# In-projection of a hybrid decoder layer: the low part of a weight tile from a DMA that adds the tile to its negated high part

## The chip, the cores and the metric

The kernel runs on one core of one Trainium2 chip. The metric is device time in microseconds (us) of one execution; less is better. TensorE (PE) does the matrix products, VectorE (DVE), ScalarE (ACT) and GpSimd (POOL) the elementwise work, and DMAs are issued by SyncE (SP) and POOL and carried by 16 DMA engines.

## The reference

One inference step of one decoder layer on 512 prompt tokens and 8 x 4 sample tokens, 544 columns in all, in float32:

```
h    = rms_norm(x, norm_mix_w)
proj = h @ w_in                      # 2048 x (7 * 1024 + 16): B_a | C_a | h_a | q | k | v | z | a | b
y_a  = rms_norm(B_a * dwconv3(C_a * h_a))                    # 8 groups of 128 channels
q, k, v = silu(dwconv4(q | k | v)), q and k L2-normalised
o    = gated_delta_rule(q, k, v, g(a), beta(b), state)       # 8 heads, chunkwise, exact
x    = x + concat(y_a, rms_norm(o) * silu(z)) @ w_out
x    = x + square(relu(rms_norm(x) @ w_up)) @ w_down         # 2048 x 8192 x 2048
y    = rms_norm(x, final_norm_w)
```

The outputs are y and the new convolution and delta states.

## The kernel before, in words

Activations lie transposed, features over 128 partitions and the 544 token columns in two halves of 272. A float32 product is made from numbers that PE takes in one pass: each operand is split into a high part, rounded to the type `fp32r`, and a low part, the rest. A product is then three: high x high, high x low, low x high (`product`).

The in-projection makes 56 slabs of 128 output features. The first three (`N_START`) are made from `w_first` while the input is still coming in. The other 53 are made one after the other, each from two weight tiles of 128 x 1024 (`w_in`, 106 tiles; the loop over `srcs`, with the tile's slab `s` and half `hf`). A tile holds 8 blocks of 128 x 128, and a block is used in 6 matmuls (3 products, 2 column halves), so a tile is 48 matmuls: for each block the two of `x_hi,w_hi`, the two of `x_lo,w_hi`, the two of `x_hi,w_lo`.

`ahead` calls `weight` two tiles ahead of the one that PE uses. `weight` loads a tile into `w_raw` (two buffers) from SP's queue, rounds it on ACT into `w_hi` (three buffers), and DVE subtracts, `w_lo = w_raw - w_hi` (three buffers).

A finished slab goes to a job: `scale_out` reads the sums on DVE, then there is a convolution (`conv`, DVE), an activation (`silu`, ACT), small copies of state on POOL (`qkv_slab`, `c_slab`, `h_slab`, `b_slab`), or a gate (`z_slab`). The 56 slabs come in four groups of 14, two heads with their q, k, v, two convolution groups, and two gates. Beside the slabs of one group runs the delta rule of the group whose q, k, v are done (`delta`, `delta_sample`, `decays`, `scalars`); these are generators, and `run_side` lets each put a few small matmuls between the slabs' own, after every second block. At a group's end `delta` normalises its output (`nk`: a logarithm and an exponential on ACT, a product on DVE, then the product with the gate on POOL, into `tmp`, and a DMA to `cat`).

Tile's scheduler orders each engine's instructions by priority and by when they could start; within `urgent()` the priority is higher, and all of `weight` stands in it. PE's order is nearly that of the program. An engine works in order: where one instruction waits, those behind it wait too. That is also true of POOL's DMA issues.

The rest of the program, the out-projection and the MLP, comes behind the in-projection (from about 830 us) and has its own weights.

Of the kernel before, what the change touches and what calls it, by code (L numbers as in the profile page):

```python
# [9 lines left out]
F32 = mybir.dt.float32  # L10
# [3 lines left out]
AF = mybir.ActivationFunctionType  # L14
ALU = mybir.AluOpType
MUL, ADD, SUB, MIN, MAX = ALU.mult, ALU.add, ALU.subtract, ALU.min, ALU.max
# [31 lines left out]
def ahead(items, load, depth=2):  # L48

    items, queue = list(items), []  # L50
    for i, it in enumerate(items):
        while len(queue) < min(depth + 1, len(items) - i):
            queue.append(load(items[i + len(queue)]))
        yield it, queue.pop(0)
# [3 lines left out]
def trunk(ctx, tc, a):  # L58
    nc = tc.nc
    V, S, G = nc.vector, nc.scalar, nc.gpsimd  # L60
# [34 lines left out]
    def tile_in(p, name, shape, dt=F32, tag=None, bufs=None):  # L95
        return p.tile(shape, dt, tag=tag or name, name=name, bufs=bufs)
# [17 lines left out]
    def urgent():  # L114
        return tc.high_priority(offset=WPRIO)
# [12 lines left out]
    def ps_big():  # L128
        t = tile_in(big, "ps_big", [P, 2, 512], tag="big")
        return [t[:, h, :HT] for h in range(2)], t[:, :, :HT]  # L130
# [1 line left out]
    def ps_small(n=512):  # L132
        return tile_in(small, "ps_sm", [P, 512], tag="sm")[:, :n]

    def weight(src, n, between=None):

        with urgent():
            raw = tile_in(rawp, "w_raw", [P, 1024])
            hi = tile_in(whip, "w_hi", [P, 1024], F32R)
            lo = tile_in(wlop, "w_lo", [P, 1024], F32R)  # L140
            for c in [slice(0, n)] if between is None else [slice(0, n // 2), slice(n // 2, n)]:
                nc.sync.dma_start(raw[:, c], src[:, c])
                S.activation(hi[:, c], raw[:, c], AF.Copy)  # L143
                if between and not c.start:
                    between()
                V.tensor_tensor(lo[:, c], raw[:, c], hi[:, c].bitcast(F32), SUB)  # L146
        return hi, lo

    def split(src, col):
# [14 lines left out]
    def product(ps, w, c, x, start, stop, halves=(0, 1)):  # L164

        (whi, wlo), (xhi, xlo) = w, x
        for i, (wp, xp) in enumerate(((whi, xhi), (whi, xlo), (wlo, xhi))):
            for h in halves:
                x = xp[h] if isinstance(xp, tuple) else xp[:, h, :]
                PE.matmul(ps[h], wp[:, c : c + P], x, start=start and i == 0, stop=stop and i == 2)  # L170
# [32 lines left out]
    with ExitStack() as mix:  # L203
# [33 lines left out]
        for kp in range(KT // 2):  # L237
# [24 lines left out]
            if kp == KT // 2 - 1:  # L262
                square_of(0)
                square_of(1)
            w = weight(a["w_first"][kp], 2 * N_START * P, None if kp else first)
            if kp == 0:
                with urgent():
# [578 lines left out]
        def run_side(drain=False):  # L846
            for item in list(side):
                if item[0] > 0 and not drain:
                    item[0] -= 1
                    continue  # L850
                while True:
                    try:
                        PE.step = True
                        item[0] = next(item[1]) - 1
                    except StopIteration:
                        side.remove(item)
                        break
                    if not drain:
                        break
            PE.step = False  # L860
# [31 lines left out]
            next(jobs)(first_ps[i])  # L892
        side.append([0, scalars()])
        srcs = [(s, hf) for s in range(56 - N_START) for hf in range(2)]
        for (s, hf), w in ahead(srcs, lambda it: weight(a["w_in"][2 * it[0] + it[1]], 1024)):
            if hf == 0:
                job = next(jobs)
                ps = ps_big()
            for k in range(8):
                kk = 8 * hf + k  # L900
                product(ps[0], w, k * P, h_x[kk], kk == 0, kk == KT - 1)
                if k % 2:
                    run_side()
            if hf == 1:
                job(ps)
# [19 lines left out]
        def add(out, ps):  # L925
            with urgent():
                V.tensor_tensor(out, out, ps, ADD)  # L927

        firsts = ahead([(o, q) for o in range(KT) for q in range(2)],
                       lambda it: weight(a["w_o1"][2 * it[0] + it[1]], N1 // 2 * P))  # L930

        def first_part(last, between):
# [36 lines left out]
    def t_tile(name, tag, dt=F32):  # L969
        return tile_in(tt, name, [P, 4, HT], dt, tag=tag, bufs=2 if tag == "u" else 1)  # L970

    def c_tile(p, name):
        return tile_in(p, name, [P, 2, HT], F32R, tag="hl" if p is hlp else "c")
# [57 lines left out]
    for (m, q), w in ahead(steps, step_weight):  # L1031
# [34 lines left out]
        if m in KEPT:  # L1066
            hi = t_tile("u_hi", "hi", F32R)
# [198 lines left out]
    while any(s < len(KS) for s in at):  # L1266
        for m in range(8):
            n = min(SPAN, len(KS) - at[m])
# [22 lines left out]
    for v, (m, k0, n) in enumerate(visits):  # L1291
        c = slice(KS[k0] * P, (KS[k0] + n) * P)
# [12 lines left out]
    for m in STORED:  # L1305
# [3 lines left out]
        for i in range(2):  # L1309
            hi, lo = c_tile(hlp, "ul"), c_tile(hlp, "ul")  # L1310
# [186 lines left out]
```

## Time and profile before

| | |
|---|---|
| time, median of 3 runs (lowest to highest) | 2399.78 us (2398.15 to 2400.69) |
| time of the profiled execution | 2399.76 us |
| its span, first to last instruction | 2398.0 us |
| busy, share of the span | PE 99%, DVE 75%, ACT 44%, POOL 19% |
| granted TensorE clock | 0.998 |
| in-projection tiles, first and last load | 27.4 and 758.8 us |

A profile page gives each engine's busy time, the chain of work that ended last, groups of instructions by line, and the DMA queues. Queries of the trace narrow these to a window of time. In a row such as `w_lo<-w_raw,w_hi` the output stands left of the arrow and the inputs right of it, by the program's names; L146 is line 146 of the kernel. "Idle before" is time in which the engine had nothing to do, and the name behind it what ended it.

### The profile page before, as it was taken

The page shows a single profiled execution, that of the slowest core. Times are in us where ns is not written, and L with a number is a line of the kernel's source. Part 1 is how long each engine was busy: PE and PEld are TensorE (multiplying, and loading weights), DVE is VectorE, ACT ScalarE, POOL GpSimd, SP SyncE. Part 2 cuts the span into 40 slices and gives each one's busy share as a digit, 9 for nine tenths or more (in the row PEclk, how much of TensorE's full clock was granted, in tenths as well). Part 3 has the DMA queues.
Part 4 walks back from the last instruction along what each step waited for, and adds up shares of the span by engine and source line. Part 5 has one row for each costly group of instructions (what it writes and reads, how often), then busy time and mean ns, then how long its engine had stood idle before and what let it go on. Part 6 is the DMA issues. An engine that isn't in the chain of part 4 may idle for free.

```text
span 2398.0 us, 47088 instructions
## 1 busy us (share of the span) xinstructions
PE 2375.6 (99%) x19089; PEld 2355.9 (98%) x19089; DVE 1788.5 (75%) x2900; ACT 1054.3 (44%) x1548; POOL 446.6 (19%) x727
## 2 busy tenths in 40 slices
PE   9999999999999999999999999999999999999997
PEld 9999999999999999999999999999999999999997
DVE  8676676666658635688888888887587887788885
ACT  6425333432532423355555555555233333333445
POOL 1233223312412302100111001111401112121003
PEclk9999999999999999999999999999999999999999
DMA  6343333333333544345555555556945657564433
GB/s 206 98 120 116 103 112 111 112 100 97 127 95 106 177 129 135 126 159 209 204 188 186 193 193 191 204 201 218 378 139 178 210 165 236 164 224 152 125 98 110
DMA packets 139889, 383.26 MB, mean 160 GB/s; under 512 B 34548, under 2 KB 43416, under 8 KB 139672
## 3 DMA queue, kind: packets, MB, share of 16 engines
q1 hardware_dynamic: 104472, 251.41, 33.2%
q0 software_dynamic: 35056, 128.82, 14.5%
q8 instruction: 150, 2.46, 0.4%
q14 instruction: 67, 0.55, 0.1%
q10 hardware_dynamic: 144, 0.03, 0.0%
HBM read 302.69 MB, written 77.49 MB: 159 GB/s over the span
## 4 chain that ended last, share of the span: by engine, by line
PE 93%; DMA 3%; DVE 2%; ACT 1%; issue 1%; POOLq 0%; SPq 0%; DVEq 0%; POOL 0%; ACTq 0%
PE ps_s L76 48%; PE ps_big L76 38%; PE ps_sm L76 7%; DMA w_q<-in_w_d_dram 1%; DMA ud<-u 1%; DVE w_lo L1130 0%; ACT w_hi L1129 0%; PE ps_sm L80 0%; DMA w_raw<-in_w_first_dram 0%; DMA w_raw<-in_w_d_dram 0%; DVE x2v L927 0%; DVE w_lo L146 0%; DVE ssq L260 0%; DMA uc<-ucd 0%; ACT w_hi L143 0%
## 5 line engine op out<-in xcount | busy, mean ns | idle before, releaser
L1129 ACT ACTIVATE w_hi<-w_q 128x768 fp32r<-128x768 f32 (+3 forms) x422 | 375.4, 890 | 559.7 <-PE ps_s L76 466.3
L76 PE MATMUL ps_s<-uc,w_hi 128*128 128x272 f32 x3136 | 592.3, 288 | 3.8 <-DVE x2v L927 1.9
L76 PEld LDWEIGHTS ps_s<-uc,w_hi 128*128 128x128 f32 x3136 | 491.2, 188 | 7.2 <-issue 3.8
L76 PE MATMUL ps_big<-x_hi,w_hi 128*128 128x272 f32 x2272 | 479.1, 292 | 0.8 <-ACT x_hi L158 0.6
L1130 DVE TENSOR_TENSOR w_lo<-w_q,w_hi 128x768 fp32r<-128x768 f32 (+3 forms) x422 | 425.5, 1009 | 72.3 <-ACT w_hi L1129 70.2
L76 PE MATMUL ps_big<-x_lo,w_hi 128*128 128x272 f32 x2272 | 472.8, 289 | 0.0
L76 PE MATMUL ps_big<-x_hi,w_lo 128*128 128x272 f32 x2272 | 470.4, 288 | 0.0
L76 PE MATMUL ps_s<-uc,w_lo 128*128 128x272 f32 x1568 | 450.5, 288 | 0.0
L143 ACT ACTIVATE w_hi<-w_raw 128x1024 fp32r<-128x1024 f32 (+3 forms) x187 | 181.7, 972 | 437.0 <-PE ps_big L76 352.4
L76 PEld LDWEIGHTS ps_big<-x_hi,w_hi 128*128 128x128 f32 x2272 | 357.1, 188 | 4.7 <-issue 1.4
L76 PEld LDWEIGHTS ps_big<-x_lo,w_hi 128*128 128x128 f32 x2272 | 357.5, 189 | 0.2 <-DVE x_lo L161 0.2
L76 PEld LDWEIGHTS ps_big<-x_hi,w_lo 128*128 128x128 f32 x2272 | 355.5, 188 | 0.3 <-DVE w_lo L146 0.2
L146 DVE TENSOR_TENSOR w_lo<-w_raw,w_hi 128x1024 fp32r<-128x1024 f32 (+3 forms) x187 | 237.7, 1271 | 106.1 <-ACT w_hi L143 97.3
L76 PEld LDWEIGHTS ps_s<-uc,w_lo 128*128 128x128 f32 x1568 | 295.1, 188 | 0.0
L76 PE MATMUL ps_s<-c_hi,w_hi 128*128 128x272 f32 x928 | 267.3, 288 | 0.4 <-ACT w_hi L1129 0.4
L76 PE MATMUL ps_s<-c_hi,w_lo 128*128 128x272 f32 x928 | 267.5, 289 | 0.0
L76 PE MATMUL ps_s<-c_lo,w_hi 128*128 128x272 f32 x928 | 266.3, 287 | 0.0
L927 DVE TENSOR_TENSOR x2v<-x2v,ps_s 128x272 f32<-128x272 f32 x326 | 140.0, 434 | 65.2 <-PE ps_s L76 64.0
L1229 POOL DMA_DIRECT2D uc<-ucd x196 | 106.6, 548 | 430.2 <-PE ps_s L76 412.7
L76 PEld LDWEIGHTS ps_s<-c_hi,w_hi 128*128 128x128 f32 x928 | 174.9, 188 | 0.7 <-ACT w_hi L1129 0.6
L76 PEld LDWEIGHTS ps_s<-c_hi,w_lo 128*128 128x128 f32 x928 | 174.3, 188 | 0.1
L76 PEld LDWEIGHTS ps_s<-c_lo,w_hi 128*128 128x128 f32 x928 | 174.4, 188 | 0.0
(371 smaller groups left out, 3754.3 us busy)
## 6 DMA issues: line engine op xcount, KB each, us to landing
w_q<-in_w_up_dram SPq DMA_DIRECT2D x116, 512.0 KB, 5.0
w_raw<-in_w_in_dram SPq DMA_DIRECT2D x106, 512.0 KB, 3.4
uc<-ucd POOLq DMA_DIRECT2D x196, 272.0 KB, 5.3
w_q<-in_w_d_dram SPq DMA_DIRECT2D x128, 384.0 KB, 3.4
ucd<-u_hi POOLq DMA_DIRECT2D x28, 544.0 KB, 5.7
ucd<-tc POOLq DMA_DIRECT2D x28, 544.0 KB, 6.8
ucd<-u_hi POOLq DMA_DIRECT2D x28, 408.0 KB, 3.0
ucd<-u POOLq DMA_DIRECT2D x28, 408.0 KB, 2.7
```

What stands on the lines that cost most here:

```text
L76: return cls.held(nc.tensor.matmul(*args, **kw))
L143: S.activation(hi[:, c], raw[:, c], AF.Copy)
L146: V.tensor_tensor(lo[:, c], raw[:, c], hi[:, c].bitcast(F32), SUB)
L927: V.tensor_tensor(out, out, ps, ADD)
L1129: S.activation(hi, s, AF.Copy)
L1130: V.tensor_tensor(lo, s, hi.bitcast(F32), SUB)
L1229: nc.gpsimd.dma_start(t.bitcast(F32), uc_d[KS[j]][:, 2 * b : 2 * b + 2])
```

## The change

For the tiles of slabs 4 and up (98 of 106) `weight` gets `by_dma=True`. ACT then writes `w_lo` itself, as the negative of the tile rounded to `fp32r`, so minus `w_hi`, and a DMA issued from POOL reads the tile from DRAM a second time and adds it to what stands in `w_lo`. DVE's subtraction is left out for these tiles.

```diff
-    def weight(src, n, between=None):
+    def weight(src, n, between=None, by_dma=False):
...
                 S.activation(hi[:, c], raw[:, c], AF.Copy)
...
-                V.tensor_tensor(lo[:, c], raw[:, c], hi[:, c].bitcast(F32), SUB)
+                if by_dma:
+                    S.activation(lo[:, c], raw[:, c], AF.Copy, scale=-1.0)
+                    nc.gpsimd.dma_start(lo[:, c], src[:, c], accum_op=ADD)
+                else:
+                    V.tensor_tensor(lo[:, c], raw[:, c], hi[:, c].bitcast(F32), SUB)
...
-        for (s, hf), w in ahead(srcs, lambda it: weight(a["w_in"][2 * it[0] + it[1]], 1024)):
+        for (s, hf), w in ahead(srcs, lambda it: weight(a["w_in"][2 * it[0] + it[1]], 1024, by_dma=it[0] >= 4)):
```

Lines behind the edit stand five lower in the changed kernel (L734 is L739 there).

The scheduler orders the engines anew. PE's order stays the same but for three places where side work moves by a few matmuls. The place that the prediction speaks of is the beginning of the second group (again in the third and the fourth): the first group's `nk` is normalised while the first tiles of the new group are made ready. ACT's order there before:

```order
L143 ACTIVATE w_hi<-w_raw 128x1024
L394 ACTIVATE gr_b<-gr_b 128x512
L102 ACT_TABLE_LOAD
L727 ACTIVATE nk<-ps_sm,epo_t 128x512 x2
L728 ACTIVATE nk<-nk 128x512
L394 ACTIVATE gr_b<-gr_b 128x512
L107 ACT_TABLE_LOAD
L107 ACTIVATE kq<-tmp 128x4x128
L107 ACTIVATE kqs<-tmp 128x28
L107 ACTIVATE kqs<-tmp 128x4
L143 ACTIVATE w_hi<-w_raw 128x1024
L728 ACT_TABLE_LOAD
```

ACT's order at the same place in the changed kernel (`gr_b` is the decay of the new group, `kq` its first q or k, `nk` the norm of the group before):

```order
L107 ACTIVATE kq<-tmp 128x4x128
L107 ACTIVATE kqs<-tmp 128x28
L107 ACTIVATE kqs<-tmp 128x4
L144 ACTIVATE w_hi<-w_raw 128x1024
L148 ACTIVATE w_lo<-w_raw 128x1024
L399 ACT_TABLE_LOAD
L399 ACTIVATE gr_b<-gr_b 128x512
L732 ACT_TABLE_LOAD
L732 ACTIVATE nk<-ps_sm,epo_t 128x512 x2
L733 ACT_TABLE_LOAD
L733 ACTIVATE nk<-nk 128x512 x2
L144 ACTIVATE w_hi<-w_raw 128x1024
```

The norm's logarithm and exponential have moved behind `kq` and behind a tile's two copies, and the place has two table loads more (the program has six more, two at each of the three places). POOL's order there before:

```order
L734 TENSOR_TENSOR tmp<-o_g,nk 128x512
L735 DMA cat_101<-tmp 256x1x256
L580 TENSOR_TENSOR qd<-qd,kq 128x512
L734 TENSOR_TENSOR tmp<-o_g,nk 128x512
L436 MEMSET tmp 128x3
L437 COPY tmp<-st 128x8x3
L735 DMA cat_102<-tmp 256x1x256
L445 COPY nst<-tmp 128x3
```

POOL's order at the same place in the changed kernel (the `w_lo` DMAs are those of three tiles that follow each other; the prediction calls the second one A and the third one B):

```order
L149 DMA w_lo<-in_w_in_dram 128x1024
L585 TENSOR_TENSOR qd<-qd,kq 128x512
L149 DMA w_lo<-in_w_in_dram 128x1024
L739 TENSOR_TENSOR tmp<-o_g,nk 128x512
L740 DMA cat_101<-tmp 256x1x256
L739 TENSOR_TENSOR tmp<-o_g,nk 128x512
L441 MEMSET tmp 128x3
L442 COPY tmp<-st 128x8x3
L149 DMA w_lo<-in_w_in_dram 128x1024
L450 COPY nst<-tmp 128x3
```

The third tile's DMA stands behind both products with `nk`, the other two ahead of them.

## The prediction

> **What bounds the kernel now.** The page's first lines come first: which engine is full.
>
> ```profile
> PE 2375.6 (99%) x19089; PEld 2355.9 (98%) x19089; DVE 1788.5 (75%) x2900; ACT 1054.3 (44%) x1548; POOL 446.6 (19%) x727
> PE ps_s L76 48%; PE ps_big L76 38%; PE ps_sm L76 7%; DMA w_q<-in_w_d_dram 1%; DMA ud<-u 1%; DVE w_lo L1130 0%; ACT w_hi L1129 0%; PE ps_sm L80 0%; DMA w_raw<-in_w_first_dram 0%; DMA w_raw<-in_w_d_dram 0%; DVE x2v L927 0%; DVE w_lo L146 0%;
> ```
>
> TensorE (PE) is busy 99% of the span, and 38% of the chain that ended last is PE's own `ps_big` products, among them the whole in-projection. VectorE (DVE), from which the change takes work, has 75%. The share is an average, so the view of busy time by windows is read next, once for the stretch in which the changed weights run and once for a part of it without side work. Columns: window, its length, then each engine's busy time; after the clock the share of the DMA engines and GB/s.
>
> ```profile
> 230.00:291.00 61.00, 61.00 (x487) 60.91 (x486) 36.75 (x47) 22.89 (x35) 17.46 (x34) 1.00 0.35 106
> 60.00:820.00 760.00, 759.79 (x6316) 749.84 (x6315) 517.31 (x1159) 290.18 (x525) 209.88 (x328) 1.00 0.36 110
> ```
>
> From 60 to 820 us PE is idle for 760.00 - 759.79 = 0.21 us, while DVE has 243 us free, ScalarE (ACT) 470, GpSimd (POOL) 550, and the DMA engines work 36% of the time. Nothing that frees DVE can gain more here than those 0.21 us. So the question is only whether the new supply of the low part still comes in time. The chain in order of time (start, us, what) gives the time that PE leaves for it:
>
> ```profile
> 230.47 60.27 PE ps_big L76 x480
> 426.74 60.27 PE ps_big L76 x480
> ```
>
> 480 matmuls are ten weight tiles of 48, so a tile lasts 6.03 us, 0.1256 us a matmul. There are three buffers for the parts of a tile: a tile's buffer comes free when the tile three before it is done, and its first low product is the fifth matmul of its own turn, 2 x 6.03 + 0.5 = 12.5 us later. This is the window for rounding, subtracting and all that takes their place. What is done in it today, by groups of instructions of the stretch (count | busy us, mean ns | idle before, its releaser):
>
> ```profile
> L146 DVE TENSOR_TENSOR w_lo<-w_raw,w_hi 128x1024 fp32r<-128x1024 f32 (+1 forms) x110 | 158.9, 1445 | 54.4 <-ACT w_hi L143 47.6 <-DMA w_raw<-in_w_in_dram 4.3
> L143 ACT ACTIVATE w_hi<-w_raw 128x1024 fp32r<-128x1024 f32 (+1 forms) x110 | 113.1, 1028 | 269.8 <-PE ps_big L76 241.3 <-issue 14.9 <-DVE xm L589 9.9
> L107 ACT ACT_TABLE_LOAD x12 | 15.4, 1283 | 0.2
> ```
>
> ACT's idle time before rounding ends on PE (241.3 us): it waits for buffers, the supply is ahead. About 2.5 us of a 12.5 us window are used.
>
> **The change part by part.** *Removed:* 98 subtractions on DVE, 98 x 1.445 = 142 us of its 517. Worth at most the 0.21 us. *Added on ACT:* 98 negated copies of the same size, 98 x 1.03 = 101 us, and six table loads of 1.28 us that the new order needs (two at each of three places, shown with the change): 290 + 109 of 760 us. *Added on POOL:* 98 issues. The nearest rows are POOL's own stores and loads; with them the transfers that bound the landing (KB each, median us from issue to landing) and the queue that carries the weights:
>
> ```profile
> L507 POOL DMA_DIRECT2D cat<-tmp x16: 682/730/787, 149.4 to 780.0; - x16
> w_raw<-in_w_in_dram SPq DMA_DIRECT2D x106, 512.0 KB, 3.4
> out_o_ss_dram<-s POOLq DMA_DIRECT2D x8, 512.0 KB, 3.2
> x2v<-x2d POOLq DMA_DIRECT2D x4, 544.0 KB, 8.0
> q1 hardware_dynamic: 104472, 251.41, 33.2%
> ```
>
> An issue is 0.73 us, 98 of them 72 us of POOL's 550 free. No row shows an adding DMA. The lower end of its landing is a plain transfer of this size: 3.2 us (store from POOL) to 3.4 us (the same tile from the SP queue). The upper end is the slowest transfer of that size on POOL's queue, 8.0 us. I take 5.0, by the nearest row, the same tile's load, and one more reading: the sum needs the 512 KB of the source and the 512 KB that stand in the destination, and q1 spends 0.332 x 16 x 2398 = 12,738 engine-us on 251.41 MB, so 0.524 MB cost 26.6 engine-us, 1.66 us over 16 engines; 3.4 + 1.66 = 5.0.
>
> The Trainium skill bears on this price. Its page "Collectives: The Full Stack", section "The bandwidth ceiling: the fold count and why AG ≠ RS ≠ AR", says that an add in the DMA path costs nothing by itself but needs two source reads, which halves the rate; the sum by the bare row would be a landing of 3.4 us, by the rule 5.0, and no run here shows an add yet.
>
> *DMA share:* 98 x 26.6 = 2,607 engine-us once, 5,214 with two readings, over 16 x 760: +0.21 or +0.43 on 0.36. Not full, 0.79 at most by these rows, but plain loads will land later. A `w_raw` load waits for its buffer, today for DVE (SP queue's own waits: us, times, longest):
>
> ```profile
> SPq L142 <- DVE w_lo L146: 376.7, 74, 9.3
> ```
>
> It is now freed by ACT's second reading, about as early as the subtraction ended, and two buffers give the load a whole turn of 6.03 us for 3.4; cost nothing, until loads take over 6 us.
>
> *Waits added:* each DMA waits at the head of POOL's queue for ACT's negation, and so for PE's buffer. Behind it stand the small copies that prepare the next slab and the products of the side work. They are due when PE ends a slab, a tile's turn or more later, so I cost that at nothing; where they stand ahead of a DMA, they cost, as follows.
>
> *The new chain.* Rounding 1.05, negating 1.05, landing 5.0: 7.1 of the 12.5 us. In the undisturbed run 10.4 us are left for the landing. It is less where ACT or POOL is late. The order of the changed program shows the worst place, the first slabs of a new head group (230 to 260 us, again at about 427 and 623). The timeline of before there (start, us, engine):
>
> ```profile
> 234.99 0.63 ACT L107 ACTIVATE kq<-tmp 128x512 f32<-128x512 f32 x1
> 235.74 1.04 ACT L143 ACTIVATE w_hi<-w_raw 128x1024 fp32r<-128x1024 f32 x1
> 238.10 0.63 ACT L728 ACTIVATE nk<-nk 128x512 f32<-128x512 f32 x1
> 239.29 1.06 ACT L143 ACTIVATE w_hi<-w_raw 128x1024 fp32r<-128x1024 f32 x1 [0.56 <-PE ps_big L76]
> ```
> ```profile
> 229.83 1.21 DVE L146 TENSOR_TENSOR w_lo<-w_raw,w_hi 128x1024 fp32r<-128x1024 f32 x1
> 232.94 0.80 DVE L423 SCALAR_TENSOR_TENSOR tmp<-tmp,cw 128x568 f32<-128x568 f32 x1
> 239.12 0.74 DVE L729 SCALAR_TENSOR_TENSOR nk<-oT,nv,nk 128x512 f32<-128x512 f32 x1
> 239.78 0.68 DVE L402 TENSOR_TENSOR tmp<-ps_big,r 128x512 f32<-128x512 f32 x1
> 242.41 0.52 DVE L421 TENSOR_SCALAR tmp<-tmp,cw 128x568 f32<-128x568 f32 x1
> ```
> ```profile
> 229.48 1.64 POOL L446 COPY nst<-tmp 128x24 f32<-128x24 f32 x1
> 239.94 1.29 POOL L734 TENSOR_TENSOR tmp<-o_g,nk 128x512 f32<-128x512 f32 x1 [1.84 <-DVE nk L729]
> 241.21 1.17 POOL L437 COPY tmp<-st 128x24 f32<-128x24 f32 x1
> 243.76 0.20 POOL L446 COPY nst<-tmp 128x24 f32<-128x24 f32 x1
> ```
> ```profile
> 245.37 0.41 PE L76 MATMUL ps_big<-x_hi,w_hi 128*128 128x272 f32 x2
> 245.88 0.41 PE L76 MATMUL ps_big<-x_hi,w_lo 128*128 128x272 f32 x2
> ```
>
> DVE reads a finished slab at 239.78, so PE began the next slab at about 239.3: its first tile, then tile A at 245.37 (first low product 245.88), then tile B, first low product 6.03 later at 251.9. A is rounded at 235.74 to 236.78; negated by 237.8, it leaves 8.0 us for its DMA. B is rounded from 239.29, but its DMA stands on POOL behind both `nk` products, and these wait for DVE's `nk` and so for ACT. On ACT the new order puts, from `kq` to the end of the first `nk`, by starts that follow each other: 0.54 and 0.21 (`kq`, `kqs`) + 0.97 + 1.07 (A's two copies) + 1.29 (load) + 0.63 + 1.3 (load) + 1.2 + 1.3 (load) + 0.63 = 9.1 us. `kq` waits for the convolution that ends at 233.7 today with a subtraction of 1.21 us ahead of it, which is gone: 232.5. So ACT is through at 241.6, DVE's `nk` (0.74) at 242.4, POOL's first product (1.3) with the issue of its store (0.3 + 0.7) at 244.7, the second (1.29) at 246.0, memset and copy (0.4 or more) at 246.4. B's DMA has 251.9 - 246.4 = 5.5 us, by the length of the copies half a microsecond more or less. With 5.0 it is just hidden, and each us of landing beyond 5.5 stalls PE a us at each of three places. The tile after B waits for the same `nk` through the next convolution, but what B lost it gains.
>
> A rule of the skill speaks against the change: "SBUF — State Buffer", section "Who interferes with whom", says that GpSimd is starved of its port while DVE runs in a two-port mode, so that DMAs issued by GpSimd stall; an estimate by it adds one such DVE operation, the 0.52 us of L421 above: 5.5 in place of 5.0, which is B's limit and still no loss. The trace agrees for copies alone: POOL's L446 copy took 1.64 us beside DVE's subtraction and 0.20 us at 243.76 without one.
>
> *The sum.* The profiled execution took 2399.76 us with a span of 2398.0; the median of the runs, 2399.78, is the same. 2399.76 - 0.2 (the idle time) + 3 x 0 to 0.5 (B's places; the landing 5.0 to 5.5, its limit 5.0 to 6.0): 2399.6 to 2401.1. I take 2400.5.
>
> **The rivals.** *One: the landing is longer than the place allows.* Slower, decided at 7.1 us: (7.1 - 5.5) x 3 = 4.8 us. For it: no row has an add, and 8.0 us is on record for a queue under load. At 8 us 2399.8 + 7.5 = 2407, at 10 us 2413. From 10.4 us on every tile of the undisturbed runs is late as well: a cycle of three buffers then takes 6.03 - 0.5 + 2.1 + L, and at L = 12 a tile takes a third of that, 6.54, 0.51 more for the 30 tiles of the three such runs (two are shown): 15 + 20 us, 2435. Against it: the same size lands in 3.2 to 3.4 from either queue in this stretch.
>
> *Two: the adding DMA is slow by rate and the engines fill up.* The first and last weight loads stand 731.4 us apart:
>
> ```profile
> L142 SPq DMA_DIRECT2D w_raw<-in_w_in_dram x106: 327/328/1613, 27.4 to 758.8; - x106
> ```
>
> A tile has 731.4 / 105 = 6.97 us on average, of which 0.36 x 6.97 = 2.5 us are taken. An add that holds the engines over 4.5 us, 2.7 times a plain load, makes DMA the bound; at 5.5 us it is 98 us: 2498. For it speaks only that nothing measured excludes it.
>
> *Three: faster.* DVE's relief reaches PE. It would need idle PE time, of which 0.21 us exist: 2399.5, no measurable gain. A real gain, over 4.8 us, would need matmuls that themselves run faster with less traffic from DVE; the 60.27 us stand unchanged in all runs of 480, whatever DVE does.
>
> **How the numbers follow.** A measurement of this kernel tells changes over 0.2%, 4.8 us. Forecast, hidden or up to 4.8 us: 0.64. Landing over 7.1 us: 0.24. Engines full: 0.09. Faster: 0.03. So same 0.64, slower 0.33, faster 0.03. The low end, 2396.5, is the lowest run shown, 2398.15, less 1.6 for a gain not seen here. The high end reaches into the first rival up to a landing of 11.2 us (2399.8 + 3 x 5.7 + 30 x 0.24 = 2424): 2425. Beyond it lie the rest of that rival and the second, some 0.14 together.
>
> **What would show it.** Right: PE idle in 60 to 820 us still under 2 us; the adding DMA 5 to 6 us from issue to landing; DVE some 140 us lower, ACT some 109 higher, POOL some 70 higher; DMA share 0.57 to 0.79. Wrong: PE idle before `x_hi,w_lo` products, released by the `w_lo` DMA, first near 252, 449 and 646 us (rival one), or in every tile with a DMA share near 1 (rival two).

## The result, and the profile after

The changed kernel takes 2435.22 us (median of 4 runs, 2430.56 to 2437.05) against 2398.97 us of the kernel before (4 runs): 1.0144 times as long, with a 95% interval of 1.0133 to 1.0156. That is 36 us slower, outside the range of the prediction. The profiled execution took 2434.5 us, with a span of 2432.7.

The page's first line, then the windows that answer to those of before (window, length, busy time of PE, PE's weight loads, DVE, ACT, POOL; granted clock, DMA share, GB/s):

```profile
PE 2387.2 (98%) x19089; PEld 2364.7 (97%) x19089; DVE 1652.6 (68%) x2802; ACT 1154.1 (47%) x1652; POOL 506.3 (21%) x825
```
```profile
230.00:291.00 61.00, 55.86 (x423) 54.64 (x423) 23.42 (x41) 37.63 (x50) 24.03 (x42) 0.97 0.79 183
60.00:860.00 800.00, 777.68 (x6363) 764.65 (x6364) 385.18 (x1071) 392.88 (x634) 273.51 (x428) 0.99 0.72 170
```

DVE did lose its work: 1788.5 - 1652.6 = 136 us less. But PE now idles 800.00 - 777.68 = 22.3 us in the stretch, where it idled 0.2, and the granted clock is 0.99 (0.97 at the start of a head group), where it was 1.00. All of the loss lies in this stretch. The same products of its last tile, before and after, stand 35.0 us apart, and the spans differ by 34.7:

```profile
799.32 0.41 PE L76 MATMUL ps_big<-x_hi,w_lo 128*128 128x272 f32 x2
```
```profile
834.32 0.41 PE L76 MATMUL ps_big<-x_hi,w_lo 128*128 128x272 f32 x2
```

What PE waited for in the in-projection (us in total, times, longest):

```profile
PE ps_big L76 <- DMA w_lo<-in_w_in_dram: 10.7, 7, 2.8
PE ps_sm L76 <- DVE y_s L797: 4.2, 1, 4.2
PE ps_sm L76 <- ACT nf L724: 4.1, 3, 1.7
PE ps_sm L76 <- POOL nl L725: 3.2, 3, 1.1
```

Only the first row is the wait that the prediction spoke of. `y_s`, `nf` and `nl` belong to the side work, the delta rule of the head group before, whose small products stand in PE's order between the weight tiles. The transfers of the stretch (KB each, median us from issue to landing), the adding DMA first, with its least, median and greatest landing; two of before, not shown yet, stand below:

```profile
DMA to landing us min/median/max: 5.2/7.9/9.3
```
```profile
w_raw<-in_w_in_dram SPq DMA_DIRECT2D x106, 512.0 KB, 4.4
gr_b<-gr SPq DMA_DIRECT2D x4, 512.0 KB, 7.8
tt<-ti SPq DMA_DIRECT2D x16, 32.0 KB, 6.0
```
```profile
gr_b<-gr SPq DMA_DIRECT2D x4, 512.0 KB, 4.7
tt<-ti SPq DMA_DIRECT2D x16, 32.0 KB, 2.8
```

The adding DMA lands in 7.9 us, not 5.0. And its neighbours are later too: the tile's load by 1.0 us, `gr_b` by 3, the small `tt` pieces by 3. How that reaches PE shows in the first head group. The timeline of POOL's and SP's queues, of ACT and of PE (start, us, what; in brackets the idle time ahead and its releaser), and SP's rows of before:

```profile
212.77 0.90 POOL L149 DMA_DIRECT2D w_lo<-in_w_in_dram  x1 [0.30 <-ACT w_lo L148]
213.37 0.86 POOL L839 DMA_DIRECT2D out_o_ss_dram<-s  x1
...
222.15 0.33 SPq L774 DMA_DIRECT2D s<-in_s_d_dram  x1
222.53 0.43 SPq L393 DMA_DIRECT2D gr_b<-gr  x1
...
230.51 1.06 ACT L395 ACTIVATE qd<-gr_b 128x1024 f32<-128x1024 f32 x1 [4.12 <-DMA gr_b<-gr]
231.48 0.61 ACT L724 ACTIVATE nf<-nk 128x512 fp32r<-128x512 f32 x1
...
232.14 0.49 PE L76 MATMUL ps_sm<-nf,ones_r 128*128 128x512 f32 x1 [1.21 <-ACT nf L724]
```
```profile
217.09 0.33 SPq L769 DMA_DIRECT2D s<-in_s_d_dram  x1
217.47 0.71 SPq L388 DMA_DIRECT2D gr_b<-gr  x1
```

The store of a state (`out_o_ss`) is issued 0.6 us behind an adding DMA on POOL's queue. SP may load the next state into that buffer only when the store has landed, which is at 222.1, 8.7 us after its issue (the median of such stores was 3.2). `gr_b` stands behind that load on SP and is issued 5 us later than before. It lands at 230.5, ACT has waited 4.12 us for it, the rounding `nf` stands behind `qd` on ACT, and PE waits for `nf`.

The clock: windows again, cut where the grant changes, and around another pause.

```profile
231.10:234.50 3.40, 1.30 (x6) 0.95 (x7) 2.89 (x9) 3.38 (x5) 2.10 (x3) 1.00 0.28 114
234.50:237.90 3.40, 3.40 (x17) 3.40 (x16) 2.93 (x6) 3.37 (x4) 1.49 (x2) 0.50 0.88 255
466.60:470.00 3.40, 2.40 (x20) 2.17 (x18) 2.66 (x4) 0.59 (x2) 1.69 (x3) 1.00 0.94 187
470.00:473.40 3.40, 1.66 (x13) 1.66 (x14) 0.00 (x0) 2.14 (x5) 0.86 (x1) 1.00 1.04 254
473.40:476.80 3.40, 3.40 (x29) 3.40 (x29) 0.00 (x0) 0.00 (x0) 0.00 (x0) 1.00 0.93 211
```

Behind the two pauses for `nf` and `nl` PE runs at half clock for 3.4 us: 17 matmuls instead of 29. A longer single pause at 469 to 472 us, 2.75 us for `w_lo`, is followed by the full clock. There are six such half-clock stretches in the in-projection (from 234.5, 439.3, 644.1, 678.2 and, two together, 790.8 us); each loses half of 3.4 us, together up to 10.2. So of the 35.0 us some 22.1 are waiting (22.3 less the 0.2 of before), some 10.2 half clock, and 1.1 stand there before the first changed tile is used (its first low product comes at 106.6 us, at 105.5 in the kernel before). The other 1.6 I do not assign.

### The profile page after: what moved, and what is told of

It reads as the page before. It is cut to its first block, busy times and chain, and to the rows that moved or that the text cites. A ratio compares the mean times of both kernels' runs of the same rounds, so it can differ in the third digit from the quotient of the medians.

```text
span 2432.7 us, 47259 instructions
## 1 busy us (share of the span) xinstructions
PE 2387.2 (98%) x19089; PEld 2364.7 (97%) x19089; DVE 1652.6 (68%) x2802; ACT 1154.1 (47%) x1652; POOL 506.3 (21%) x825
## 4 chain that ended last, share of the span: by engine, by line
PE 75%; issue 11%; DMA 6%; DVE 3%; ACT 2%; POOL 2%; SPq 1%; POOLq 0%; DVEq 0%; ACTq 0%
PE ps_s L76 40%; PE ps_big L76 29%; PE ps_sm L76 6%; DMA w_lo<-in_w_in_dram 1%; DMA out_o_ss_dram<-s 1%; DMA gr_b<-gr 1%; DVE xm L594 1%; DVE tm L590 1%; DMA w_q<-in_w_d_dram 0%; POOL ucd L1185 0%; POOL ucd L1184 0%; DMA ti<-xm 0%; ACT w_lo L148 0%; ACT w_hi L144 0%; PE ps_sm L80 0%
## 5 line engine op out<-in xcount | busy, mean ns | idle before, releaser
L76 PE MATMUL ps_big<-x_hi,w_lo 128*128 128x272 f32 x2272 | 474.6, 290 | 10.7 <-DMA w_lo<-in_w_in_dram 10.7
L76 PE MATMUL ps_s<-d_hi,w_hi 128*128 128x272 f32 x464 | 133.9, 288 | 0.4 <-ACT u L1200 0.4
```

The source lines that it names most:

```text
L76: return cls.held(nc.tensor.matmul(*args, **kw))
```

## The experiments

Theory A, formed from this trace, says that there are three losses. The adding DMA lands too late for `w_lo` (10.7 us); it delays other transfers on which the side work depends (`nf`, `nl`, `y_s`, 11.5 us); and pauses of PE cost clock on top (10.2 us). The rivals are named in the expectations. All times stand against runs of the kernel before on the same chip, and each ratio has its 95% interval.

**ACT's copy alone.**

```diff
                     S.activation(lo[:, c], raw[:, c], AF.Copy, scale=-1.0)
-                    nc.gpsimd.dma_start(lo[:, c], src[:, c], accum_op=ADD)
+                    V.tensor_tensor(lo[:, c], raw[:, c], hi[:, c].bitcast(F32), SUB)
```

> ACT's negated copy stays in all 98 tiles, and DVE's subtraction then overwrites it as before; no second DMA. Theory A: ACT's 102 us lie in its idle time, PE idles under 1 us in the in-projection, 2399 to 2402 us. Rival C (ACT's copies and its 6 more table loads delay the exponentials, the square roots and the roundings that PE waits for at the head groups): the waits on nf and nl remain, 2406 us or more.

2399.96 us, ratio 1.0000 (0.9991 to 1.0009). PE idles 0.2 us in its in-projection. The copies cost nothing. The six table loads are not tested here: ACT has 98 instructions more than before (1646 against 1548), not 104 (1652) as after the change, and its order at the head groups is nearly that of before. They are in the next kernel.

**The same DMA without the add.**

```diff
-                    nc.gpsimd.dma_start(lo[:, c], src[:, c], accum_op=ADD)
+                    nc.gpsimd.dma_start(lo[:, c], src[:, c])
```

> The kernel after, with the second DMA as a plain copy of the tile (no add; the low part is then the whole tile, so the output is not the reference's). Theory A (the add makes each packet long, 347 against 178 ns, so that the landing is 7.9 us and the neighbours on the queues are late): without the add a packet takes about 200 ns, the DMA lands in 4 to 5.5 us, the DMA share falls from 0.72 to about 0.56, PE's waits on w_lo go, and the time is 2399 to 2408 us. Rival B (any second DMA of the tile, with its 51 MB and its issue on POOL, costs this): landing 7 us or more, time over 2422 us.

2404.84 us, 1.0023 (1.0014 to 1.0033). Its landing and PE's waits on it, and POOL's queue in this kernel, after the change and before (packets, MB, share of the 16 engines):

```profile
w_lo<-in_w_in_dram POOLq DMA_DIRECT2D x98, 512.0 KB, 4.8
```
```profile
PE ps_big L76 <- DMA w_lo<-in_w_in_dram: 0.8, 3, 0.4
```
```profile
q0 software_dynamic: 49168, 180.20, 20.8%
```
```profile
q0 software_dynamic: 49168, 180.20, 26.3%
```
```profile
q0 software_dynamic: 35056, 128.82, 14.5%
```

The same bytes without the add land in 4.8 us, and PE waits 0.8 us in all: 0.4 us for the prediction's tile B at 251.6 us, and in the next two groups 0.2 us each for the tile behind B, at 454.1 and 650.7 us (B itself lands there 0.1 us before its use). Rival B is out. ACT has all 1652 instructions of the changed kernel here, the six table loads among them, so these cost next to nothing as well, and rival C is out. q0's shares of 16 spans, 8,003 engine-us here, 10,237 after the change and 5,563 before, give (8,003 - 5,563) / 98 = 25 engine-us for a plain copy of a tile and (10,237 - 5,563) / 98 = 48 for the adding one. From 60 to 820 us a 4096-byte packet of this queue, packets of its other transfers included, took 347 ns on average with the add and 192 without. In the profiled run the in-projection ends within 0.3 us of that of before; what this kernel loses lies behind it, among it two waits of PE in later parts (at 1088 and 1777 us, 2.1 us each), the second followed by a half-clock stretch. Why these waits are longer there I did not find.

**The DMA beside the subtraction, into a tile that nobody reads.** Two forms; in the first the negated copy comes from `w_raw`, ahead of the subtraction, in the second from `w_hi`, behind it. The edit of the second:

```diff
-                    S.activation(lo[:, c], raw[:, c], AF.Copy, scale=-1.0)
-                    nc.gpsimd.dma_start(lo[:, c], src[:, c], accum_op=ADD)
+                    V.tensor_tensor(lo[:, c], raw[:, c], hi[:, c].bitcast(F32), SUB)
+                    scr = tile_in(xep, "w_scr", [P, 1024], F32R, tag="xe")
+                    S.activation(scr[:, c], hi[:, c].bitcast(F32), AF.Copy, scale=-1.0)
+                    nc.gpsimd.dma_start(scr[:, c], src[:, c], accum_op=ADD)
```

> The kernel after with DVE's subtraction back for w_lo; ACT's negated copy and the adding DMA go to a scratch tile that nobody reads. Theory A (three separate losses: waits on w_lo 10.7 us, waits of the side chains on other DMAs that the adding one delays 11.5 us, the clock's drops after the pauses about 10 us): the waits on w_lo go, those on nf, nl and y_s and their drops stay: 2412 to 2422 us. Rival D (everything follows from the late w_lo; the side waits come from the shifted order): 2399 to 2404 us.

> As the first scratch kernel, but the negated copy is made from w_hi behind DVE's subtraction, so that ACT meets nothing ahead of the rounding and w_raw is held no longer than before. Theory A: no wait on w_lo, the waits of side chains on gr_b, tt and the stores stay, and so do part of the drops: 2408 to 2422 us. Rival D (late w_lo is the cause of all): 2399 to 2404 us.

The first took 2452.95 us, 1.0225 (1.0208 to 1.0242), slower than the change itself: a miss of the experiment. Its negated copy needs no buffer that PE frees, so the order puts it ahead on ACT, where it holds everything behind it until the next tile has landed:

```profile
ACT w_scr L149 <- DMA w_raw<-in_w_in_dram: 255.2, 78, 8.1
```

It therefore says nothing on the theories. The second took 2415.58 us, 1.0063 (1.0047 to 1.0080). No wait on `w_lo` is left, and PE still waits for the side work, here for `tn`, which comes with `tt` from the same small transfers:

```profile
PE ps_sm L76 <- DVE tn L610: 10.4, 4, 4.2
```
```profile
tt<-ti SPq DMA_DIRECT2D x16, 32.0 KB, 7.7
```

Rival D, that all of it comes from the late `w_lo`, is out: this kernel loses 15 us though nobody waits for the adding DMAs themselves. Three of its four waits on `tn` (near 177, 376 and 577 us) stand where the changed kernel did not wait for the side work, as the order moved. So it shows that these DMAs cost time beside `w_lo`, and not how much of the 36 us that is.

**More room for `w_lo`.** Each fourth tile takes its `w_hi` and `w_lo` from a pool that is not used before the out-projection, and weights are fetched three tiles ahead.

```diff
-            hi = tile_in(whip, "w_hi", [P, 1024], F32R)
-            lo = tile_in(wlop, "w_lo", [P, 1024], F32R)
+            turn[0] += 1
+            xe = by_dma and turn[0] % 4 == 3
+            hi = tile_in(xep if xe else whip, "w_hi", [P, 1024], F32R, tag="xe" if xe else None)
+            lo = tile_in(xep if xe else wlop, "w_lo", [P, 1024], F32R, tag="xe" if xe else None)
...
-        for (s, hf), w in ahead(srcs, lambda it: weight(a["w_in"][2 * it[0] + it[1]], 1024, by_dma=it[0] >= 4)):
+        for (s, hf), w in ahead(srcs, lambda it: weight(a["w_in"][2 * it[0] + it[1]], 1024, by_dma=it[0] >= 4), 3):
```

> The kernel after with four buffers of w_hi and w_lo and the weights fetched three tiles ahead in place of two, so that a tile has about 18.5 us from its first free buffer to its use. Theory A: PE waits on w_lo go (10.7 us and some 2 us of clock), the side chains' waits stay: 2417 to 2425 us. Rival D (late w_lo is the cause of all): 2399 to 2404 us. Rival E (the DMA engines are near full, so that more room does not help): 2430 us or more.

2419.47 us, 1.0085 (1.0070 to 1.0100). The DMA still lands in 7.9 us, and no wait on `w_lo` is left; those on `y_s`, `nf` and `nl` are still there:

```profile
PE ps_sm L76 <- DVE y_s L801: 3.2, 1, 3.2
PE ps_sm L76 <- POOL nl L729: 2.1, 2, 1.1
PE ps_sm L76 <- ACT nf L728: 2.1, 2, 1.2
```

Not all of this kernel's loss lies in the in-projection: in the profiled run, 18.7 us longer than before, the in-projection ends 13.8 us later, and two half-clock stretches fall behind it (from 1693.2 and 1792.1 us).

**The state's store off POOL's queue.**

```diff
-                nc.gpsimd.dma_start(a["o_ss"][2 * gi + hl], s1)
+                nc.sync.dma_start(a["o_ss"][2 * gi + hl], s1)
```

> The kernel after with the eight stores of the sample states (o_ss) issued on SP in the place of POOL, so that they no longer stand behind an adding DMA on its queue. Theory I (SP waits for that store before it can load the next state and, behind it, gr_b): the store lands in under 5 us, PE's waits on nf and nl (7.3 us) and their half-clock stretches (three, 5.1 us) go: 2421 to 2427 us. Rival F (all transfers are late because the engines are shared with the adding packets, whichever queue they are on): the store still takes over 7 us, 2431 to 2438 us.

2426.82 us, 1.0114 (1.0095 to 1.0133). The store lands in 5.0 us, `gr_b` in 5.5, and the waits on `nf` and `nl` are gone; what is left:

```profile
PE ps_big L76 <- DMA w_lo<-in_w_in_dram: 12.7, 8, 2.8
PE ps_sm L76 <- DVE y_s L797: 5.1, 4, 3.6
```

The chain over the store was the cause of these waits. The clock's share did not go with them: the in-projection still has five half-clock stretches in place of six, behind other pauses. Both edits together:

> Four buffers with the weights fetched three tiles ahead, and the o_ss stores on SP, together. Theory A: the waits on w_lo, nf and nl are gone, only the one on y_s by the late tt loads is left, with its drop: 2405 to 2413 us. Rival: the two edits relieve the same loss, and together give no more than the better one alone (depth 2419.5 us): 2417 to 2421 us.

2407.71 us, 1.0036 (1.0022 to 1.0049). Against the kernel before on its own chip the change loses 36.3 us, more room 19.3, the moved store 26.2, and both together 8.5. So the gains add up, 16.9 and 10.1 us alone and 27.8 together, with 98 adding DMAs still in place. In the profiled run (2404.36 us, the fastest of four) this wait is left:

```profile
PE ps_sm L76 <- DVE y_s L801: 3.0, 1, 3.0
```

With one on `at` (1.3 us, another product of the side work) and one half-clock stretch (1.7 us) it makes 6.0 of the 6.4 us by which the in-projection is longer there.

**The source of the add in SBUF** (`w_raw`, of which there are four buffers here).

```diff
-                    nc.gpsimd.dma_start(lo[:, c], src[:, c], accum_op=ADD)
+                    nc.gpsimd.dma_start(lo[:, c], raw[:, c], accum_op=ADD)
```

> The kernel after with w_raw in SBUF as the source of the adding DMA in the place of the tile in DRAM (four w_raw buffers, so that the longer hold costs no load). If the second reading of DRAM makes the transfer long: a packet of the adding queue takes under 250 ns, it lands in under 6 us, and the time is 2400 to 2412 us. If the add itself (reading its target and writing it) does: 330 to 380 ns, 7 to 9 us, 2425 to 2440 us.

2412.99 us, 1.0059 (1.0044 to 1.0074), just outside the first case. The landing is 5.3 us, so 2.6 of the 7.9 come with reading the tile from DRAM a second time; but a packet still takes 331 ns and q0's share is 25.9%, so the long packet comes with the add, from either source. Both halves of the expectation are partly right. PE still waits 4.9 us for `w_lo`.

**Where, or how many.** The adding DMA for 58 tiles, outside the slabs in which PE had waited, and the other way round (`in` for `not in`) for the 40 tiles of these slabs.

```diff
-        for (s, hf), w in ahead(srcs, lambda it: weight(a["w_in"][2 * it[0] + it[1]], 1024, by_dma=it[0] >= 4)):
+        for (s, hf), w in ahead(srcs, lambda it: weight(a["w_in"][2 * it[0] + it[1]], 1024, by_dma=it[0] >= 4 and (it[0] + N_START) % 14 not in (0, 1, 2, 3, 11, 12))):
```

> The kernel after with the adding DMA for 58 of the 98 tiles, those of slabs 4 to 10 and 13 of each head group's 14; slabs 0 to 3, 11 and 12, where PE's waits were, keep DVE's subtraction. Theory A with places (the loss sits where the side chain's own transfers, or the shortest windows, meet the adding DMA): 2398 to 2405 us, PE idle under 4 us in the in-projection. Rival J (the loss goes with the number of adding DMAs): 58/98 of 36 us, 2419 to 2424 us.

> The other half: the adding DMA only for the 40 tiles of slabs 0 to 3, 11 and 12, DVE's subtraction for the other 58. Theory A with places: most of the loss, 2420 to 2438 us. Rival J: 40/98 of 36 us, 2412 to 2417 us.

With 58 adding DMAs 2403.06 us, 1.0018 (1.0009 to 1.0027); with the 40 others 2434.43 us, 1.0144 (1.0131 to 1.0158), all of the loss. Window and landing of the first, window and waits of the second (both from 60 to 820 us):

```profile
60.00:820.00 760.00, 756.89 (x6287) 746.11 (x6286) 435.03 (x1096) 344.06 (x581) 245.01 (x385) 1.00 0.60 149
```
```profile
w_lo<-in_w_in_dram POOLq DMA_DIRECT2D x58, 512.0 KB, 7.9
```
```profile
60.00:820.00 760.00, 737.83 (x6042) 724.69 (x6041) 428.10 (x1064) 318.37 (x540) 223.20 (x355) 0.99 0.50 131
```
```profile
PE ps_big L76 <- DMA w_lo<-in_w_in_dram: 14.6, 9, 2.5
```

The 58 land no sooner, in 7.9 us, and load the DMA engines more (0.60 against 0.50), but no product waits for them. They still cost 3.8 us; in the profiled run, 3.0 us longer than before, 2.9 are three waits on `y_s`. Place decides, not number; rival J is out.

**The last wait.** To the two edits together, DVE's subtraction for the 24 tiles of slabs 10 to 12.

```diff
-        for (s, hf), w in ahead(srcs, lambda it: weight(a["w_in"][2 * it[0] + it[1]], 1024, by_dma=it[0] >= 4), 3):
+        for (s, hf), w in ahead(srcs, lambda it: weight(a["w_in"][2 * it[0] + it[1]], 1024, by_dma=it[0] >= 4 and (it[0] + N_START) % 14 not in (10, 11, 12)), 3):
```

> Four buffers, weights three tiles ahead, the o_ss stores on SP, and DVE's subtraction back for the 24 tiles of slabs 10 to 12 of each group, whose adding DMAs run beside the tn and tt loads; the other 74 of the 98 tiles keep the adding DMA. Theory A (three places, nothing else): the last wait, on y_s by the late tt loads, goes as well; PE idles under 1.5 us in the in-projection, 2398 to 2402.5 us, no longer different from before. Rival J (what is left of the loss goes with the number of adding DMAs): 74/98 of the 8.5 us that the two edits alone left: 2405 to 2407 us.

2410.14 us, 1.0040 (1.0027 to 1.0054): a miss of both. `tt` does land in 2.7 us now, but PE still waits 2.5 us for `y_s` at 761 us, and DVE's row ahead of it names another cause:

```profile
757.77 1.21 DVE L155 TENSOR_TENSOR w_lo<-w_raw,w_hi 128x1024 fp32r<-128x1024 f32 x1
760.35 0.54 DVE L430 TENSOR_SCALAR tmp<-tmp,cw 128x560 f32<-128x560 f32 x1 [1.37 <-POOL tmp L478]
760.80 0.28 DVE L801 TENSOR_TENSOR y_s<-ps_sm,rq 128x128 f32<-128x128 f32 x1
```

In this order `y_s` stands behind a subtraction and a convolution that waits for POOL. After the change, DVE's row ahead of the same `y_s` was a wait for the late `tt`:

```profile
790.45 0.45 DVE L608 STREAM_TRANSPOSE tn<-tn 128x256 f32<-128x256 f32 x1 [8.55 <-DMA tt<-ti]
```

So the wait on `y_s` came from late transfers after the change, as that trace has it, but it has another cause here, and theory A is not complete: that an earlier `tt` alone would end this wait is not shown, and what this kernel and the one with the two edits still lose, 8.5 to 10 us, is explained only in part.

**The clock by itself.** The kernel before, with the subtraction of eight tiles repeated.

```diff
-                V.tensor_tensor(lo[:, c], raw[:, c], hi[:, c].bitcast(F32), SUB)
+                for _ in range(times):
+                    V.tensor_tensor(lo[:, c], raw[:, c], hi[:, c].bitcast(F32), SUB)
```

> The kernel before, with DVE's subtraction of eight weight tiles, 49 us apart, repeated 9 to 20 times, so that PE has to wait for these w_lo for lengths from nothing to some 10 us; it measures the clock alone. Theory G (the clock is set on a fixed grid of 3.413 us, as the starts of all the drops after the change are multiples of it apart; a stretch of the grid in which PE idles more than about 1.8 us is followed by one at half clock): pauses that a grid line cuts into parts under 1.6 us cost nothing more, longer ones cost one stretch for each such stretch; all drops start on the grid. Rival H (the length of the pause alone decides): every pause over 1.5 us is followed by a drop, at whatever time it falls.

2484.08 us in one run. Two stretches of the grid ahead of a drop, and the drop:

```profile
288.40:291.80 3.40, 1.86 (x15) 1.64 (x14) 3.37 (x3) 0.14 (x1) 1.96 (x1) 1.00 0.48 154
291.80:295.20 3.40, 0.74 (x4) 0.55 (x4) 3.40 (x5) 0.92 (x1) 2.68 (x3) 1.00 0.00 0
295.20:298.60 3.40, 2.97 (x13) 2.97 (x14) 3.40 (x5) 0.00 (x0) 0.44 (x3) 0.50 0.47 129
```

With 1.5 us idle in the first, nothing follows; with 2.7 in the second, the third is at half clock. Over the eleven traces that show such drops (43 of them, the change's own included, the beginning and the end of each run left out), all starts of a trace lie on one grid of 3.4133 us, to 3 ns. Of the grid's stretches at full clock, all 31 in which the records show PE idle 1.9 us or more are followed by half clock, 9 of 19 with 1.55 to 1.9, and 3 of 95 with 0.5 to 1.55. Theory G holds, with a band of about 0.35 us in which it does not decide: a pause that a grid line cuts into parts under 1.55 us is nearly always free of this cost, one of 1.9 us within a stretch is not. The 2.75 us above were cut into 1.0 and 1.74, so that they went free was in part luck.

## Why the prediction was wrong

- *Nothing to gain from DVE:* right. DVE lost 136 us, and no variant was faster.
- *ACT's 109 us hidden:* right (100 measured), by the runs with ACT's copy alone and without the add. POOL's issue took 0.89 us instead of 0.73 (the rows below), and that is 88 us of POOL's idle time, not of PE's.

```profile
L148 ACT ACTIVATE w_lo<-w_raw 128x1024 fp32r<-128x1024 f32 x98 | 102.2, 1043 | 0.0
L149 POOL DMA_DIRECT2D w_lo<-in_w_in_dram x98 | 87.6, 894 | 189.7 <-ACT w_lo L148 161.6 <-ACT ke_s L756 24.2 <-issue 3.0
```

- *Landing 5.0 us:* wrong, 7.9. The engine time was well foreseen: 48 engine-us for an adding DMA (53 foreseen) against 25 for the plain one, and the DMA share was 0.72, inside 0.57 to 0.79. So the trace agrees with the halved rate that the Trainium skill, "Collectives: The Full Stack", section "The bandwidth ceiling: the fold count and why AG ≠ RS ≠ AR", gives for the add of a ring collective. The step that failed adds that engine time to the landing of an undisturbed transfer, 3.4 us. The plain copy behind POOL's queue already took 4.8 in this traffic, from SBUF the add took 5.3, and from DRAM 7.9.
- *Tile B's 5.5 us, and three times each us beyond it:* the place was right, the limit and the price were not. PE was ready for B at 258.62 - 1.32 = 257.30 (POOL's and PE's rows for B and for the tile behind it stand below), so B's DMA had 4.6 us in place of 5.5, and as much in the next two groups: from `kq`'s start to B's use it was 18.8 us instead of 19.4, to B's issue 14.2 instead of 13.9. B landed after 5.9, 5.5 and 5.4 us, sooner than the median, and cost 1.3, 0.9 and 0.8 us, 3.1 together. The tile behind B was costed at nothing, because what B lost it gains. With that gain it had 5.3 to 5.8 us, landed after 7.3, 8.1 and 8.0, and cost 1.6, 2.8 and 2.8 us, 7.1 together. A seventh pause, 0.5 us at 380.9, hit another tile. That the prediction's price at the median, 3 x (7.9 - 5.5) = 7.2 us, makes two thirds of the 10.7 measured is luck, as it puts all of it on B.

```profile
252.70 1.02 POOL L149 DMA_DIRECT2D w_lo<-in_w_in_dram  x1
258.62 0.52 PE L76 MATMUL ps_big<-x_hi,w_lo 128*128 128x272 f32 x2 [1.32 <-DMA w_lo<-in_w_in_dram]
259.17 0.88 POOL L149 DMA_DIRECT2D w_lo<-in_w_in_dram  x1 [1.90 <-ACT w_lo L148]
266.48 0.52 PE L76 MATMUL ps_big<-x_hi,w_lo 128*128 128x272 f32 x2 [1.56 <-DMA w_lo<-in_w_in_dram]
```

- *The rule on GpSimd's port:* the row that the prediction sets beside it, L446, shows a POOL copy beside DVE's subtraction, and not beside an operation such as L421's. No run here tests whether DVE held up B's DMA.
- *Loads and queue neighbours cost nothing:* this is the larger failure. The text looked at what stands behind the adding DMA on POOL as an engine, and at `w_raw`, but not at POOL's stores as transfers, nor at who waits for their landing. The store, SP's load behind it, `gr_b` and `nf` make 7.3 us of waiting (shown by the run with the store on SP), `y_s` 4.2 (by the trace alone).
- *No term for the clock:* 10.2 us, nearly as much as the waits on `w_lo`. Pauses were priced at their length.

So the first rival had one of the three mechanisms, and at a landing of 8 us it gave 2407: it lacked 28 us, of which 11.5 are the side work's waits, 10.2 the clock, 3.2 more waiting on `w_lo` (10.7 against its 7.5), 1.1 from before the first changed tile, and the rest is not assigned.

## What to carry to other kernels

Before moving work onto a queue, list every transfer on that queue and on those that wait for a landing there, not only the instructions behind it on the engine; a landing is priced in the traffic of its own stage and not from a quiet row. A late supply hurts at a few places only: find the shortest window, and change the rest of the tiles alone, as the 58 of 98 tiles show (here even these gained nothing, as DVE was not the bound). Price a pause of TensorE with the clock that may be lost after it.

## What was not expected of the hardware

- With the add a 4096-byte packet of POOL's queue took 347 ns against 192 for the plain copy, and 331 with the source in SBUF in place of DRAM, while the landing differs by 2.6 us between the two sources.
- A plain store issued 0.6 us behind an adding DMA on the same queue landed after 8.7 to 8.8 us at all three beginnings of a group. Behind the plain copy at that place it took 6.0 to 6.3, issued on SP 4.9 to 5.0, and in the kernel before 3.3 to 3.6.
- POOL's issue of the adding DMA took 0.87 us (median), that of the plain copy 0.55.
- TensorE's clock is set on a fixed grid of 3.4133 us, and one stretch with some half of it idle halves the next. The free-running window of this length stands in the Trainium skill, "TensorE: Matmul & The Clock Gate", section "What's actually happening", and the traces agree. That pauses must exceed about 3.4 us, as its section "HAM oscillation — how this bites in real kernels" says, they do not bear out: 1.9 us within one stretch were enough in 31 cases of 31.
